# Sums over partitions of the second layer's modulation chunks, issued in the middle of the next chunk

## The chip, the cores and the metric

One core of a Trainium2 chip runs the whole kernel. The metric is the device time of one launch in microseconds (us); three runs of the kernel before gave 2981.88, 2982.76 and 2983.58 us. TensorE is PE here, VectorE is DVE, ScalarE is ACT, GpSimd is POOL, SyncE is SP; SP issues most of the loads from memory.

## The reference, cut to what matters

Two layers over 1024 latent tokens and 256 context tokens of width 1024. Each layer takes six modulation vectors for the latents (from `c`) and six for the context (from `c_ctx`) out of a product of a 1024-vector with a 1024 x 6144 matrix.

```python
def adaln(cond, w, b):
    m = jax.nn.silu(cond) @ w + b
    return jnp.split(m[..., None, :], 6, axis=-1)
...
for i in range(DEPTH):
    sh1, sc1, g1, sh2, sc2, g2 = adaln(c, ada_w[i], ada_b[i])
    csh1, csc1, cg1, csh2, csc2, cg2 = adaln(c_ctx, ada_w[i], ada_b[i])
    hx = modulate(rmsnorm(x, norm1_g[i]), sh1, sc1)
    ...
    x = x + g1 * yx
    x = x + g2 * sq_relu_mlp(modulate(rmsnorm(x, norm2_g[i]), sh2, sc2), mlp_w1[i], mlp_w2[i])
```

In the last layer only two of the context's vectors are needed, so of the second layer's 24 chunks of 256 columns the first 8 are made for both conditions and the other 16 for `c` alone.

## The kernel before, in words

The kernel is one stream of work per engine in an order written out by hand; no scheduler moves anything. The first layer's MLP (`mlp(0, ...)`, about 490 to 1480 us) is where the second layer's modulations are made beside the matmuls.

**The MLP.** Every matmul of it is three (`mm3`, L341 to L343: high x high, high x low, low x high). After three first up-projections it runs in passes. A pass is `down` of two rows of hidden channels, then two `up`s. `down` goes over three blocks of tokens (latents 0 to 511, latents 512 to 1023, the 256 context tokens), in each over 8 output tiles d; a group of 6 matmuls fills one PSUM bank, the banks 2, 3, 4, 5 in turn, and DVE adds each bank into the residual (`xL` for latents, `xC` for context; this is called an eviction below). The PE can therefore be four groups ahead of DVE's evictions and no more. `up` has 24 matmuls for each of the three blocks, in banks 0 and 1, which ACT empties. The weights come through `Stream`: a raw 512 KB load into a tile of ring R (three tiles), a high part by ACT and a low part by POOL into ring W (L333, L337; a split), after which the next raw load is issued.

**Background steps.** `later("ada", ada_dve(1))` hands in a Python generator, and `step()` runs it up to its next `yield`. `down` calls `step()` after every second d, `up` once after each block. So a pass has 18 steps; below they are named by place: a1 to a4 in `down` of the first latents, b1 to b4 in that of the second latents, c1 to c4 in that of the context, u1 to u3 after the three blocks of the first `up`, u4 to u6 after those of the second. What a step issues stands on each engine's queue behind what was issued ahead of it.

**A chunk** (`ada_dve`, L516 to L552) takes 9 steps: (1) take an accumulator from ring Y (three tiles) and load the first half of its weights into a tile of R (L525); (2), (3) DVE multiplies and adds that half into the accumulator, two of four slices in each step (in the trace `Y<-R,k` and `Y<-R,k,Y`, 4 instructions a step for two conditions and 2 for one; DVE instructions of the helpers all have L296); (4) load the second half; (5), (6) the same for it; (7) nothing; (8) the sums over partitions: matmuls of the accumulator with a column of ones into bank 7 (L543, 4 matmuls for two conditions and 2 for one; the trace counts each as two); (9) DVE adds the bias and stores the result (`k<-bank,k`, called the placing below), and once in four chunks POOL makes scale vectors from it (`fin_mod`).

Two chunks of 9 steps are one pass of 18, so each pass looks like the one before. The even chunk has its sums at a4. The odd one has step 1 at b2, steps 2 and 3 at b3 and b4, step 4 at c1, steps 5 and 6 at c2 and c3, and its sums at u1.

R's loads are issued by SP in the order of the program. A load waits until the last reader of the tile it overwrites is done: a DVE instruction where that held modulation weights, a POOL split where it held a raw weight.

Of the kernel before, what the change touches and what calls it, by code (L numbers as in the profile page):

```python
# [13 lines left out]
ALU = mybir.AluOpType  # L14
# [187 lines left out]
class Kern:  # L202
# [312 lines left out]

    def ada_dve(self, layer):  # L516

        nc, I = self.nc, self.I
        for chunk in range(24):
            conds = (0, 1) if chunk < 8 else (0,)  # L520
            n = len(conds)
            acc = self.Y.v(2, 256)
            for kh in range(2):
                w = self.R.v(4, 256)
                nc.sync.dma_start(out=w, in_=I["ada_w"][layer, 512 * kh:512 * kh + 512,  # L525
                                                        256 * chunk:256 * chunk + 256]
                                  .rearrange("(k p) c -> p k c", p=128))
                yield
                for k in range(4):
                    for c in conds:  # L530
                        s = self.cs[:, 4 * kh + k, c:c + 1]
                        if kh + k == 0:
                            self.ts(acc[:, c], w[:, k], s, ALU.mult)
                        else:
                            self.stt(acc[:, c], w[:, k], s, acc[:, c], ALU.mult, ALU.add)
                    if k == 1:
                        yield
                yield
            yield
            ps = self.PS[7]  # L540
            for j in range(2):
                for c in conds:
                    nc.tensor.matmul(ps[:, 2 * j + c:2 * j + c + 1], lhsT=acc[:, c, 128 * j:128 * j + 128],  # L543
                                     rhs=self.ones[:, 0:1], start=True, stop=True)
            yield
            d0 = 2 * chunk % 8
            for c in conds:
                self.tt(self.modc[:, layer, c, chunk // 4, d0:d0 + 2], ps[:, c:c + 3:2],
                        self.adab[:, layer, 2 * chunk:2 * chunk + 2], ALU.add)
            if chunk % 4 == 3:  # L550
                self.fin_mod(layer, chunk // 4, conds)
            yield  # L552


    def exp_small(self, o, x, tmp):
# [1594 lines left out]
```

## Time and profile before

| what | value |
|---|---|
| median of three runs | 2982.76 us (2981.88 to 2983.58) |
| the profiled execution: its time | 2984.72 us |
| the profiled execution: its span | 2982.9 us, mean granted clock 0.984 |
| PE busy | 2868.5 us, 96% |
| DVE busy | 1764.3 us, 59% |
| POOL busy | 1148.5 us, 39% |
| ACT busy | 1028.6 us, 34% |

The span is the time from the first to the last recorded instruction; 1.8 us of the profiled execution's time lie around it. PE is busy nearly always, so a microsecond is won where PE stands idle or where its clock is granted at the lower of its two levels (1.2 and 2.4 GHz; a granted clock of 0.50 is the lower, 1.00 the upper).

### The profile page before, as it was taken

How to read it: one execution, taken by the hardware profiler on the slowest of the kernel's cores; microseconds unless marked ns; L12 is line 12 of the kernel's file. 1: busy time of each engine (PE TensorE's matmuls, PEld its weight loads, DVE VectorE, ACT ScalarE, POOL GpSimd, SP SyncE). 2: the span in 40 equal slices, each digit the busy share in tenths (PEclk: the TensorE clock that was granted, in tenths of full speed). 3: DMA queues.
4: the chain of work that ended last, by engine and by line, in shares of the span. 5: the costliest groups of instructions: out<-in, count | busy, mean ns of one | idle time of the engine just before them, and what ended most of it. 6: DMA issues, size and time to landing. Idle time of an engine off the chain costs nothing.

```text
span 2982.9 us, 39200 instructions
## 1 busy us (share of the span) xinstructions
PE 2868.5 (96%) x15186; PEld 2390.5 (80%) x15186; DVE 1764.3 (59%) x3533; ACT 1028.6 (34%) x1799; POOL 1148.5 (39%) x842
## 2 busy tenths in 40 slices
PE   5899999999999999999999999999999999999999
PEld 2666788788888888888778788999887888888887
DVE  7789867644554454332779847999966322332233
ACT  3342343222122212212334435666644223223221
POOL 5613233422223223323434425787724333333332
PEclk8898999999999999999999999999999999999999
DMA  7265530222212222111155642322222111111111
GB/s 287 90 192 164 189 109 17 64 64 64 71 64 85 73 69 81 62 36 43 40 160 163 159 126 89 101 82 84 77 93 65 54 50 50 50 43 57 44 49 71
DMA packets 179035, 263.30 MB, mean 88 GB/s; under 512 B 8736, under 2 KB 125984, under 8 KB 178336
## 3 DMA queue, kind: packets, MB, share of 16 engines
q1 hardware_dynamic: 168208, 233.53, 25.0%
q0 software_dynamic: 10640, 27.26, 3.0%
q8 instruction: 119, 1.95, 0.3%
q14 instruction: 68, 0.56, 0.1%
HBM read 210.92 MB, written 49.84 MB: 87 GB/s over the span
## 4 chain that ended last, share of the span: by engine, by line
PE 73%; DVE 18%; ACT 3%; DMA 3%; issue 2%; POOL 2%; SPq 0%; DVEq 0%; ACTq 0%; POOLq 0%
PE bank L341 19%; PE bank L342 19%; PE bank L343 19%; PE sc L1686 4%; PE pv L1726 4%; DVE Y L296 3%; DVE T L895 2%; DVE E L296 2%; PE tb L1717 2%; DVE xh L899 2%; DMA R<-in_ada_w_dram 1%; DVE hl L296 1%; DVE S L296 1%; DVE R L296 1%; DVE xL L296 1%
## 5 line engine op out<-in xcount | busy, mean ns | idle before, releaser
L296 DVE SCALAR_TENSOR_TENSOR xL<-bank,k,xL 128x512 f32<-128x512 f32 x544 | 404.5, 749 | 905.0 <-PE bank L343 904.7
L337 POOL TENSOR_TENSOR W<-R,W 128x1024 fp32r<-128x1024 f32 (+1 forms) x138 | 330.6, 2406 | 684.6 <-ACT W L333 395.8
L341 PE MATMUL bank<-H,W 128*128 128x512 f32 (+1 forms) x1280 | 473.5, 370 | 2.2 <-DVE xC L296 2.2
L342 PE MATMUL bank<-H,W 128*128 128x512 f32 (+1 forms) x1280 | 471.0, 368 | 0.0
L343 PE MATMUL bank<-H,W 128*128 128x512 f32 (+1 forms) x1280 | 471.0, 368 | 0.0
L333 ACT CAST W<-R 128x1024 fp32r<-128x1024 f32 (+2 forms) x180 | 178.2, 1009 | 667.8 <-PE bank L343 363.6
L337 POOL TENSOR_TENSOR H<-E,H 128x512 fp32r<-128x512 f32 (+1 forms) x160 | 190.8, 1193 | 476.3 <-ACT H L333 462.3
L341 PE MATMUL bank<-hl,W 128*128 128x512 f32 (+1 forms) x768 | 303.6, 395 | 8.1 <-ACT hl L433 3.8
L342 PE MATMUL bank<-hl,W 128*128 128x512 f32 (+1 forms) x768 | 299.1, 389 | 6.6 <-DVE hl L296 5.6
L343 PE MATMUL bank<-hl,W 128*128 128x512 f32 (+1 forms) x768 | 296.8, 386 | 1.1 <-DVE W L337 1.1
L341 PEld LDWEIGHTS bank<-H,W 128*128 128x128 f32 x1280 | 241.3, 189 | 43.5 <-DVE xC L296 3.4
L343 PEld LDWEIGHTS bank<-H,W 128*128 128x128 f32 x1280 | 241.2, 188 | 40.5
L342 PEld LDWEIGHTS bank<-H,W 128*128 128x128 f32 x1280 | 241.4, 189 | 39.8 <-issue 0.2
L1453 ACT ACTIVATE E<-bank 128x512 f32<-128x512 f32 (+1 forms) x160 | 88.8, 555 | 491.8 <-PE bank L343 491.8
L1691 DVE TENSOR_REDUCE S<-sc 128x1 f32<-128x1280 f32 x128 | 184.2, 1480 | 38.9 <-PE sc L1686 38.9
L341 PEld LDWEIGHTS bank<-hl,W 128*128 128x128 f32 x768 | 148.8, 194 | 59.1 <-issue 19.2
L296 DVE SCALAR_TENSOR_TENSOR Y<-R,k,Y 128x256 f32<-128x256 f32 x224 | 166.4, 773 | 28.3 <-DMA R<-in_ada_w_dram 25.7
L342 PEld LDWEIGHTS bank<-hl,W 128*128 128x128 f32 x768 | 148.5, 193 | 39.2 <-DVE hl L296 11.5
L343 PEld LDWEIGHTS bank<-hl,W 128*128 128x128 f32 x768 | 147.9, 193 | 29.7 <-DVE W L337 1.5
L1686 PE MATMUL sc<-K,W 128*128 128x512 f32 x720 | 167.7, 369 | 0.0
L1726 PE MATMUL pv<-xL,wT 128*128 128x128 f32 x1280 | 155.8, 275 | 0.0
L324 POOL TENSOR_TENSOR R<-R,S 128x896 f32<-128x896 f32 x64 | 107.4, 1678 | 112.0 <-DVE S L296 87.5
(387 smaller groups left out, 5960.4 us busy)
## 6 DMA issues: line engine op xcount, KB each, us to landing
R<-in_w_dram SPq DMA_DIRECT2D x128, 512.0 KB, 3.6
R<-in_ada_w_dram SPq DMA_DIRECT2D x52, 512.0 KB, 3.6
W<-q_d POOLq DMA_DIRECT2D x15, 1024.0 KB, 5.5
A<-in_ada_w_dram SPq DMA_DIRECT2D x24, 512.0 KB, 4.4
hl<-in_ada_w_dram SPq DMA_DIRECT2D x20, 512.0 KB, 9.7
kk_d<-T SPq DMA_DIRECT2D x20, 512.0 KB, 3.2
K<-kk_d POOLq DMA_DIRECT2D x8, 1280.0 KB, 6.2
R<-in_od_in_dram SPq DMA_DIRECT2D x18, 512.0 KB, 3.7
```

Source lines behind the costliest of these rows:

```text
L296: f(**kw)
L324: self.nc.gpsimd.tensor_tensor(out=o, in0=a, in1=b, op=op)
L333: nc.scalar.copy(hi, src)
L337: e.tensor_tensor(out=lo, in0=src, in1=hi.bitcast(F32), op=ALU.subtract)
L341: mm(ps, lhsT=lh, rhs=rh, start=first, stop=False)
L342: mm(ps, lhsT=lh, rhs=rl, start=False, stop=False)
L343: mm(ps, lhsT=ll, rhs=rh, start=False, stop=last)
L895: v.tensor_tensor(out=b.raw(o, [[48, 2], [1, 32]]), in0=self.CAb.raw(64 * d, [[32, 2], [1, 32]]), in1=h.raw(prev[d], [[0, 2], [1, 32]]), o ...
L1453: self.nc.scalar.activation(out=e, in_=ps, func=AF.Relu)
L1686: nc.tensor.matmul(self.SC[i][:, c0:c0 + n], lhsT=Qf[:, e, q0:q0 + 128], rhs=K[:, i, c0:c0 + n], start=e == 0, stop=e == 1)
L1691: nc.vector.tensor_reduce(out=st[:, i, 1:2], in_=self.SC[i][:, 0:1280], axis=AX.X, op=ALU.max, negate=True)
L1726: nc.tensor.matmul(self.PV[:, 0:128], lhsT=it["wT"][:, kt], rhs=heads[h]["v"][:, kt], start=kt == 8, stop=kt == 3)
```

## The change

A chunk's sums and placing are taken out of the chunk and done in the next one. The sums stand at the end of the step after the next chunk's step 3, the placing at the head of the first step that works on the next chunk's second half. The empty step 7 and the two steps that held only the sums and the placing go, one empty step comes at the end, so a chunk has 8 steps and not 9: (1) load, (2), (3) the first half, (4) the sums of the chunk before, (5) load, (6) the placing of the chunk before and the second half's first two slices, (7) the other two, (8) nothing. A 25th turn without work of its own sums and places the last chunk. The instructions are the same ones, as many as before on each engine, with the same operands.

```diff
+        late = None
+
+        def sums(acc, conds):
+            ps = self.PS[7]
+            for j in range(2):
+                for c in conds:
+                    nc.tensor.matmul(ps[:, 2 * j + c:2 * j + c + 1], lhsT=acc[:, c, 128 * j:128 * j + 128],
+                                     rhs=self.ones[:, 0:1], start=True, stop=True)
+
+        def place(chunk, conds):
+            d0 = 2 * chunk % 8
+            for c in conds:
+                self.tt(self.modc[:, layer, c, chunk // 4, d0:d0 + 2], self.PS[7][:, c:c + 3:2],
+                        self.adab[:, layer, 2 * chunk:2 * chunk + 2], ALU.add)
+            if chunk % 4 == 3:
+                self.fin_mod(layer, chunk // 4, conds)
+
+        for chunk in range(25):
...
                 yield
-                for k in range(4):
+                if late and kh:
+                    place(late[0], late[2])
+                    late = None
+                for k in range(4) if chunk < 24 else ():
...
                     if k == 1:
                         yield
                 yield
-            yield
-            ps = self.PS[7]
-            for j in range(2):
-                for c in conds:
-                    nc.tensor.matmul(ps[:, 2 * j + c:2 * j + c + 1], lhsT=acc[:, c, 128 * j:128 * j + 128],
-                                     rhs=self.ones[:, 0:1], start=True, stop=True)
-            yield
-            d0 = 2 * chunk % 8
...
-            yield
+                if late:
+                    sums(late[1], late[2])
+                yield
+            late = (chunk, acc, conds)
```

With 8 steps a chunk and 18 a pass, nine chunks fill four passes, and the places move from pass to pass. The sums of chunks 0 to 8 stand at b4 and u4 of the first pass, b2 and u2 of the second, a4 and c4 of the third, a2, c2 and u6 of the fourth; then it begins anew. All 24 chunks take 198 steps and not 216, so the generator ends one pass earlier.

PE, first pass, around the end of the first `up`'s first block, before (`bank1_7` is the bank of the sums, `Y51_8` the accumulator of chunk 1, `hl` the normed latents, `W12_29` and `W12_30` the two `up`s' weights):

```order
L341 MATMUL bank1_1_61<-hl_47_3675,W12_29_4967 128x512
L342 MATMUL bank1_1_61<-hl_47_3675,W12_29_4967 128x512
L343 MATMUL bank1_1_61<-hl_47_3675,W12_29_4967 128x512
L543 MATMUL bank1_7_67<-k_7_94,Y51_8_5070 128x1 x4
L341 MATMUL bank1_0_60<-hl_48_3679,W12_29_4967 128x512
```

The same sums after the change, on PE around the end of the second `up`'s first block:

```order
L341 MATMUL bank1_0_60<-hl_47_3675,W12_30_5175 128x512
L342 MATMUL bank1_0_60<-hl_47_3675,W12_30_5175 128x512
L343 MATMUL bank1_0_60<-hl_47_3675,W12_30_5175 128x512
L526 MATMUL bank1_7_67<-k_7_94,Y51_8_5050 128x1 x4
L341 MATMUL bank1_1_61<-hl_48_3679,W12_30_5175 128x512
```

Chunk 1's sums moved from u1 to u4, three blocks of `up` later on PE.

DVE, second pass, at the seam of the second latents and the context (b4 to c2), before (`xL` and `xC` rows are evictions, `Y51_10` is chunk 3's accumulator, `R13_52` and `R13_53` its two halves of weights):

```order
L296 SCALAR_TENSOR_TENSOR xL_37_2870<-bank1_4_64,k_9_102,xL_37_2870 128x512
L296 SCALAR_TENSOR_TENSOR xL_37_2870<-bank1_5_65,k_9_102,xL_37_2870 128x512
L296 SCALAR_TENSOR_TENSOR Y51_10_5486<-R13_52_5487,k_11_110,Y51_10_5486 128x256 x4
L296 SCALAR_TENSOR_TENSOR xC_38_2874<-bank1_2_62,k_9_102,xC_38_2874 128x256
L296 SCALAR_TENSOR_TENSOR xC_38_2874<-bank1_3_63,k_9_102,xC_38_2874 128x256
L296 SCALAR_TENSOR_TENSOR xC_38_2874<-bank1_4_64,k_9_102,xC_38_2874 128x256
L296 SCALAR_TENSOR_TENSOR xC_38_2874<-bank1_5_65,k_9_102,xC_38_2874 128x256
L296 SCALAR_TENSOR_TENSOR Y51_10_5486<-R13_53_5539,k_11_110,Y51_10_5486 128x256 x4
```

The same seam after the change:

```order
L296 SCALAR_TENSOR_TENSOR xL_37_2870<-bank1_4_64,k_9_102,xL_37_2870 128x512
L296 SCALAR_TENSOR_TENSOR xL_37_2870<-bank1_5_65,k_9_102,xL_37_2870 128x512
L296 TENSOR_TENSOR k_9_102<-bank1_7_67,k_3_76 128x2 x2
L296 SCALAR_TENSOR_TENSOR Y51_10_5438<-R13_53_5509,k_11_110,Y51_10_5438 128x256 x4
L296 SCALAR_TENSOR_TENSOR xC_38_2874<-bank1_2_62,k_9_102,xC_38_2874 128x256
L296 SCALAR_TENSOR_TENSOR xC_38_2874<-bank1_3_63,k_9_102,xC_38_2874 128x256
L296 SCALAR_TENSOR_TENSOR Y51_10_5438<-R13_53_5509,k_11_110,Y51_10_5438 128x256 x4
L296 SCALAR_TENSOR_TENSOR xC_38_2874<-bank1_4_64,k_9_102,xC_38_2874 128x256
L296 SCALAR_TENSOR_TENSOR xC_38_2874<-bank1_5_65,k_9_102,xC_38_2874 128x256
```

A placing and four accumulator instructions now stand ahead of the first context eviction, and four more ahead of the third; before, four stood ahead of the first and the next four behind the fourth.

DVE, third pass, in the first latents (a2 and the evictions behind it), before:

```order
L296 SCALAR_TENSOR_TENSOR xL_37_2870<-bank1_5_65,k_9_102,xL_37_2870 128x512
L296 SCALAR_TENSOR_TENSOR Y51_11_5694<-R13_58_5797,k_11_110,Y51_11_5694 128x256 x4
L296 SCALAR_TENSOR_TENSOR xL_37_2870<-bank1_2_62,k_9_102,xL_37_2870 128x512
L296 SCALAR_TENSOR_TENSOR xL_37_2870<-bank1_3_63,k_9_102,xL_37_2870 128x512
L296 SCALAR_TENSOR_TENSOR xL_37_2870<-bank1_4_64,k_9_102,xL_37_2870 128x512
```

The same place after the change (`Y51_12` is chunk 5):

```order
L296 SCALAR_TENSOR_TENSOR xL_37_2870<-bank1_5_65,k_9_102,xL_37_2870 128x512
L296 TENSOR_SCALAR Y51_12_5826<-R13_60_5827,k_11_110 128x256 x2
L296 SCALAR_TENSOR_TENSOR Y51_12_5826<-R13_60_5827,k_11_110,Y51_12_5826 128x256 x2
L296 SCALAR_TENSOR_TENSOR xL_37_2870<-bank1_2_62,k_9_102,xL_37_2870 128x512
L296 SCALAR_TENSOR_TENSOR xL_37_2870<-bank1_3_63,k_9_102,xL_37_2870 128x512
L296 SCALAR_TENSOR_TENSOR Y51_12_5826<-R13_60_5827,k_11_110,Y51_12_5826 128x256 x4
```

The end of chunk 4 stood here before; now chunk 5 begins here. Its load (`R13_60`) goes into a tile of R that a raw weight held, and waits for the POOL split of that weight, the one at the head of the pass.

## Rows read from the trace of the kernel before

**Rows 1.** The page: span, instructions; PE busy (share) x instructions, PEld, DVE, ACT, POOL.

```profile
span 2982.9 us, 39200 instructions
PE 2868.5 (96%) x15186; PEld 2390.5 (80%) x15186; DVE 1764.3 (59%) x3533; ACT 1028.6 (34%) x1799; POOL 1148.5 (39%) x842
```

**Rows 2.** PE's waits, 550 to 800, then 800 to 1262: us, times, longest us.

```profile
PE bank L543 <- DVE Y L296: 14.7, 4, 3.7
```

```profile
PE bank L543 <- DVE Y L296: 5.2, 8, 0.7
```

**Rows 3.** PE by pass: window, us, busy (instructions), granted clock, DMA share, GB/s.

```profile
550.50:614.40 63.90, 60.28 (x306) 0.95 0.23 74
...
863.20:920.30 57.10, 56.43 (x299) 1.00 0.24 74
...
1262.40:1317.50 55.10, 55.10 (x291) 1.00 0.13 39
```

**Rows 4.** PE behind the four long waits, the same columns.

```profile
588.48:594.42 5.94, 5.94 (x18) 0.50 0.27 88
594.42:600.00 5.58, 5.58 (x34) 1.00 0.27 97
652.44:659.27 6.83, 6.83 (x20) 0.50 0.24 79
717.30:724.12 6.82, 6.82 (x20) 0.50 0.23 77
782.15:785.56 3.41, 3.41 (x11) 0.50 0.47 154
```

**Rows 5.** PE's timeline: start us, us, instruction, count [idle before <- releaser].

```profile
561.43 0.95 PE L543 MATMUL bank<-k,Y 128*128 128x1 f32 x8
...
573.27 0.28 PE L341 MATMUL bank<-H,W 128*128 128x256 f32 x1
...
573.98 0.28 PE L341 MATMUL bank<-H,W 128*128 128x256 f32 x1
...
588.48 1.86 PE L543 MATMUL bank<-k,Y 128*128 128x1 f32 x8 [3.62 <-DVE Y L296]
```

```profile
1239.70 0.61 PE L543 MATMUL bank<-k,Y 128*128 128x1 f32 x4 [0.67 <-DVE Y L296]
```

**Rows 6.** DVE's timeline in the first pass, the same columns.

```profile
554.52 3.31 DVE L296 SCALAR_TENSOR_TENSOR Y<-R,k,Y 128x256 f32<-128x256 f32 x4 [0.33 <-DMA R<-in_ada_w_dram]
...
565.98 0.21 DVE L296 TENSOR_TENSOR k<-bank,k 128x2 f32<-128x2 f32 x2
...
569.39 0.75 DVE L296 SCALAR_TENSOR_TENSOR xL<-bank,k,xL 128x512 f32<-128x512 f32 x1 [0.61 <-PE bank L343]
570.75 0.75 DVE L296 SCALAR_TENSOR_TENSOR xL<-bank,k,xL 128x512 f32<-128x512 f32 x1 [0.61 <-PE bank L343]
...
574.14 1.67 DVE L296 SCALAR_TENSOR_TENSOR Y<-R,k,Y 128x256 f32<-128x256 f32 x4
575.72 1.66 DVE L296 SCALAR_TENSOR_TENSOR xC<-bank,k,xC 128x256 f32<-128x256 f32 x4
579.46 5.99 DVE L296 SCALAR_TENSOR_TENSOR Y<-R,k,Y 128x256 f32<-128x256 f32 x4 [2.08 <-DMA R<-in_ada_w_dram]
...
586.16 2.67 DVE L296 SCALAR_TENSOR_TENSOR Y<-R,k,Y 128x256 f32<-128x256 f32 x4
```

**Rows 7.** Accumulator instructions, then latent evictions: duration ns min/median/max, first and last start.

```profile
L296 DVE SCALAR_TENSOR_TENSOR Y<-R,k,Y x224: 468/484/2673, 538.2 to 1237.1; 128x256 f32<-128x256 f32 x112
```

```profile
L296 DVE SCALAR_TENSOR_TENSOR xL<-bank,k,xL x192: 733/750/753, 552.1 to 1227.9; 128x512 f32<-128x512 f32 x192
```

**Rows 8.** POOL's timeline: weight splits in the first pass and at the second's head.

```profile
580.24 4.92 POOL L337 TENSOR_TENSOR W<-R,W 128x1024 fp32r<-128x1024 f32 x2 [23.88 <-ACT W L333]
```

```profile
617.01 2.40 POOL L337 TENSOR_TENSOR W<-R,W 128x1024 fp32r<-128x1024 f32 x1 [0.27 <-ACT W L333]
```

**Rows 9.** The page's loads: count, KB, median us to landing.

```profile
R<-in_ada_w_dram SPq DMA_DIRECT2D x52, 512.0 KB, 3.6
```

**Rows 10.** Waits 550 to 1262 of SP's queue, then 760 to 1250 of ACT.

```profile
SPq L149 <- DVE Y L296: 43.5, 19, 3.0
```

```profile
ACT W L333 <- PE bank L343: 229.0, 9, 25.8
```

More of the change, by code (lines that the diff above doesn't have):

```diff
@@ L518, in ada_dve @@
         nc, I = self.nc, self.I
-        for chunk in range(24):
+        late = None
[13 more added lines that the diff above has]
+        for chunk in range(25):
             conds = (0, 1) if chunk < 8 else (0,)
-            n = len(conds)
-            acc = self.Y.v(2, 256)
+            if chunk < 24:
+                acc = self.Y.v(2, 256)
             for kh in range(2):
[L524 to L527, printed above, removed]
+                if chunk < 24:
+                    w = self.R.v(4, 256)
+                    nc.sync.dma_start(out=w, in_=I["ada_w"][layer, 512 * kh:512 * kh + 512,
+                                                            256 * chunk:256 * chunk + 256]
+                                      .rearrange("(k p) c -> p k c", p=128))
                 yield
-                for k in range(4):
+                if late and kh:
+                    place(late[0], late[2])
+                    late = None
+                for k in range(4) if chunk < 24 else ():
                     for c in conds:
@@ L538, in ada_dve @@
                 yield
-            yield
-            ps = self.PS[7]
-            for j in range(2):
-                for c in conds:
-                    nc.tensor.matmul(ps[:, 2 * j + c:2 * j + c + 1], lhsT=acc[:, c, 128 * j:128 * j + 128],
-                                     rhs=self.ones[:, 0:1], start=True, stop=True)
-            yield
-            d0 = 2 * chunk % 8
[L547 to L551, printed above, removed]
-            yield
+                if late:
+                    sums(late[1], late[2])
+                yield
+            late = (chunk, acc, conds)
     def exp_small(self, o, x, tmp):
```

## The prediction

> **What bounds the kernel now.** I read the page first: PE is busy for 2868.5 of 2982.9 us [rows 1], so only PE's idle time and its clock can give anything. Then PE's waits over the stretch in which the chunks are made. One line stands there: the sums (L543) waited 12 times for DVE's accumulator, four times for 14.7 us together and eight times for 5.2 us [rows 2], 19.9 us in all. Then the windows by pass: the first pass takes 63.90 us at a granted clock of 0.95, a pass whose chunks have one condition 57.10 us at 1.00, and a pass without chunks 55.10 us, busy all the time [rows 3]. So the chunks cost PE 8.8 us in a pass with two conditions and 2.0 us in one with one. Last, PE's timeline at one of the long waits: 3.62 us of idle time, then the eight records of the sums take 1.86 us where the same eight took 0.95 us at 561.43 us [rows 5]. The window behind it shows why: granted clock 0.50, the lower level, for 5.94 us, and 1.00 again after it [rows 4].
>
> DVE's timeline tells where the 3.6 us come from [rows 6]. Four accumulator instructions at b4 end at 575.8 us, four context evictions follow, and then the second half of the odd chunk waits for its load, which could only start when b4's four had freed a tile of R. It begins at 579.46 us, needs 5.99 us for four instructions that take 1.67 us elsewhere, since two weight splits run on POOL from 580.24 us for 4.92 us [rows 8], and the last four start at 586.16 us. PE got to the sums at u1 3.6 us too early. With one condition the same chain is half as long, and the wait is 0.67 us [rows 5].
>
> **What the change removes.** (1) The 12 waits: the sums of a chunk now stand five steps behind the chunk's last DVE step. The shortest such stretch is chunk 5's, whose last DVE step is b3 and whose sums stand at c4: PE has two latent groups between, at 1.36 us (evictions that wait for PE follow each other at 569.39 and 570.75 us [rows 6]), and eight context groups at 0.71 us (573.27 to 573.98 us [rows 5]), 8.4 us. DVE was late by 3.7 us at most [rows 2]. So I take all 19.9 us as gone. (2) The low clock behind the long waits. From the sums on it lasts 5.94, 6.83, 6.82 and 3.41 us [rows 4], 23.0 us at half speed, which is 11.5 us lost. It began each time with a wait of 3.6 to 3.7 us, and not once with the eight short ones (the pass at 863.20 us has 1.00 [rows 3]), so it goes with the long waits. Together 31.4 us.
>
> What stays: the sums themselves, 24 of them, with as many instructions as before. A pass with one condition is 57.1 - 55.1 - 0.65 (5.2 us by 8 waits) = 1.35 us dearer than one without chunks, two sums' worth of 0.7 us. They interrupt PE wherever they stand, so nothing is won or lost by where; and they still write bank 7, which no MLP matmul uses.
>
> **What it moves.** Loads: the 48 loads are the same ones, but each now stands elsewhere among the raw weights' loads in SP's queue. What hides them: SP's raw loads waited up to 3.0 us for DVE to free a tile of R, and ACT's splits were nevertheless held by PE, up to 25.8 us, and not by loads [rows 10]. A raw load can be late by that much before PE sees it, so I cost this at nothing; if the cover went, PE would wait for a weight, with a half clock behind it. The placing on DVE now waits for the sums of two steps ago. Behind it in DVE's queue stand accumulator instructions and evictions; two steps of PE lie between, so it finds its bank ready. POOL's `fin_mod` waits for the placing of chunks 7 and 19 alone, with weight splits queued behind it, and PE is then at c4 and u6, where DVE is at most a few short instructions behind: nothing.
>
> What is new is where the accumulator instructions meet the evictions, since PE can be only four groups ahead. A group of four takes 1.58 us (574.14 to 575.72), a context eviction 0.4 us, a latent one 0.75 us [rows 6]. Two places with two conditions come out short:
> - Second pass, the seam b4/c1 (chunk 3). PE starts the context at time 0. In the trace the last latent eviction is done 0.87 us later (573.27 [rows 5] to 574.14 [rows 6]). Then the placing 0.2 us [rows 6], four accumulator instructions 1.58 us, and the first context eviction ends at 3.1 us. PE's fifth group wants that bank at 4 x 0.71 = 2.84 us: a wait of 0.3 us. Four more accumulator instructions put the third eviction's end at 5.55 us, and PE's seventh group wants it at 4.5 us: 1.0 us. Sum 1.3 us.
> - Third pass, a2 (chunk 5). The load waits for POOL's split. In the second pass that ends 5.0 us after the pass's start (617.01 + 2.40 [rows 8], start 614.40 [rows 3]); the load lands 3.6 us later [rows 9], four instructions make it 10.2 us, the eviction 10.95 us. PE's ninth group wants it at 8 x 1.36 = 10.9 us: 0.1 us. The next eviction and four more instructions make it 13.2 us and the third eviction 13.95 us, where PE's eleventh group wants its bank at 13.6 us: 0.3 us. Sum 0.4 us.
>
> With one condition these groups have half the length, and the same working leaves no wait. New waits: 1.7 us. No row shows either place. The lower bound is nothing; below nothing it can't be, since in the present order the waits of this stretch name the sums alone [rows 2] and no eviction. The upper bound is a half clock behind each of the two, 3.4 us each by the longest of rows 4, so 8.5 us. I take 1.7 us: the short waits of rows 2 are the nearest in length, and they cost their own length.
>
> The accumulator instructions stretch beside POOL: 484 ns in the median, 2673 ns at most, while the latent evictions stay within 733 to 753 ns [rows 7]. The Trainium skill (SBUF — State Buffer, section "SBUF: two separate sides") has a rule that speaks against moving them into `down`: the port pair that DVE shares with GpSimd is locked for a whole instruction, and a DVE instruction with two SBUF inputs stands still until the GpSimd one is done. The trace agrees: four took 5.99 us against POOL's 4.92 us. By that rule every group at a1 or a2 could be held for a split's 2.40 us with evictions behind it; if that came on top at both places above, the sum would be 4.8 us higher, where by the rows the split has ended before chunk 5's load starts.
>
> **The sum.** Against the profiled execution, 2984.72 us (span 2982.9 us and 1.8 us around it): -19.9 - 11.5 + 1.7 = -29.7, so 2955.0 us. That execution lies 2.0 us above the median of the runs, so on their scale 2953 us.
>
> **The rivals.**
> - New short waits bring the clock down. The 1.3 us at chunk 3 or the 0.4 us at chunk 5 is enough, or a third place falls short: 3.4 us for each, 2953 + 3.4 to 2953 + 10. For it: the new waits stand beside other broken stretches. Against it: eight waits of 0.65 us left the clock at 1.00 [rows 2, 3]. The Trainium skill (TensorE: Matmul & The Clock Gate, section "A second HAM failure mode: psum-queue depth-cycling") says that frequent small gaps between groups of matmuls, as banks are cycled, can make the clock swing; no row here shows it.
> - Only part of the gain: the one-condition waits or the low clock come back at other places. 2964 to 2976 us, by keeping the 11.5 us or more.
> - The change doesn't do what it says: DVE is still writing the accumulator when PE comes to the new place. It decides from a lag of 8.4 us on; the rows show 3.7. Then the 12 waits and their clock stay: within 6 us of 2983.
> - Slower: DVE's queue becomes PE's limit in `down`. Place: a group of four at a1 to b4 with evictions behind it. PE has four groups, 5.45 us; less the eviction ahead and the one behind, a group may take some 3.8 us. The group at 554.52 us took 3.31 us beside POOL [rows 6] and cost PE nothing; one of 5.99 us there would cost 2.2 us and, as with rows 4, some 3 us of clock. If two places in each of 11 passes crossed it, 22 x 5 = 110 us against 31: about 3060 us; to end slower by 0.2% it takes eight such places. Against it: POOL's long pairs of splits run at c and u1, and only one split at the head of `down`.
>
> **How the numbers follow.** Forecast 0.64, clock at new waits 0.20, part of the gain 0.07, no effect 0.05, slower 0.04. The range: 2949 us (no new wait, 2951.4, less the scatter of the runs) to 2964 us (both new places with a half clock, 2960, and one more of 3.6 us); it leaves out the last three. Measured here, 0.2% or 6 us is about what can be told from no change: faster 0.91, same 0.05, slower 0.04.
>
> **What would show it.** In the changed kernel's profile the line of the sums waiting for DVE is gone from PE's waits. The granted clock is 1.00 in every pass with chunks, and a pass with two conditions takes 58 to 59 us. A line of PE waiting for DVE's `xC` or `xL` appears, with 1 to 3 us in total, the largest at the seam of the second pass. I am wrong if that line holds 6 us or more, if the clock falls behind it, or if PE waits for `W`.

## The result and the profile after

The changed kernel takes 2952.75 us in the median of four runs (2950.45 to 2954.23), the kernel before 2982.32 us in four: a ratio of 0.9889, interval 0.9877 to 0.9902. It is 1.1% faster; 2953 us was forecast. The profiled execution took 2952.55 us against 2984.72 us, 32.2 us less.

The page of the changed kernel, the first two lines as in [rows 1]:

```profile
span 2950.8 us, 39233 instructions
PE 2854.7 (97%) x15186; PEld 2384.6 (81%) x15186; DVE 1732.3 (59%) x3533; ACT 1028.4 (35%) x1799; POOL 1149.0 (39%) x842
```

The engines run the same instructions as before (the 33 more in the count are not on these five lines). PE is busy 13.8 us less, for the most part since the matmuls behind the long waits no longer run slowly, and the span is 32.1 us shorter, so some 18 us of PE's idle time went.

PE's waits between 549 and 1229 us, the stretch of the passes with chunks, which answer to [rows 2]: engine, line, what it waited for, us in all, times, longest.

```profile
PE bank L341 <- DVE xL L296: 1.1, 1, 1.1
PE bank L341 <- DVE xC L296: 0.7, 1, 0.7
```

No line of the sums is left. Two waits for evictions came in their place, 1.8 us together.

PE by pass, the columns of [rows 3]: window, us, busy (instructions), granted clock, DMA share, GB/s.

```profile
549.60:608.10 58.50, 57.41 (x305) 1.00 0.24 82
608.10:666.40 58.30, 57.54 (x307) 1.00 0.26 82
666.40:723.30 56.90, 56.90 (x306) 1.00 0.24 75
723.30:780.60 57.30, 57.30 (x310) 1.00 0.26 83
780.60:836.80 56.20, 56.20 (x299) 1.00 0.24 76
...
1173.60:1228.70 55.10, 55.10 (x290) 1.00 0.14 39
```

The clock is 1.00 in each of them, where the first four passes had 0.95 to 0.97; the fourth of the kernel before, which [rows 3] leaves out, was this:

```profile
743.30:806.20 62.90, 59.19 (x306) 0.97 0.21 68
```

A pass with two conditions takes 56.9 to 58.5 us and not 62.9 to 64.6 us, one with one condition 56.0 to 56.4 us and not 57.0 to 57.1 us, and the generator ends a pass earlier.

The stretch from the first pass to the end of the passes, 14 of them, in the kernel before and in the changed one:

```profile
550.52:1372.57 822.05, 802.10 (x4161) 0.99 0.21 67
```

```profile
549.65:1338.91 789.26, 787.42 (x4162) 1.00 0.22 70
1338.91:2950.80 1611.89, 1584.13 (x8256) 0.99 0.27 80
```

The passes are 32.8 us shorter. Ahead of them 0.9 us is gained, behind them 1.6 us lost (2982.9 - 1372.57 = 1610.3 us before), which is less than the runs of one kernel differ by. So the whole result lies where the change is.

### The profile page after: what moved, and what is told of

Read it like the earlier page. It is cut to its first block, busy times and chain, and to the rows that moved or that the text cites. A ratio compares the mean times of both kernels' runs of the same rounds, so it can differ in the third digit from the quotient of the medians.

```text
span 2950.8 us, 39233 instructions
## 1 busy us (share of the span) xinstructions
PE 2854.7 (97%) x15186; PEld 2384.6 (81%) x15186; DVE 1732.3 (59%) x3533; ACT 1028.4 (35%) x1799; POOL 1149.0 (39%) x842
## 4 chain that ended last, share of the span: by engine, by line
PE 81%; DVE 9%; issue 3%; ACT 3%; POOL 2%; DMA 2%; SPq 0%; DVEq 0%; ACTq 0%; POOLq 0%
PE bank L341 22%; PE bank L342 21%; PE bank L343 21%; PE sc L1698 4%; PE pv L1738 4%; PE tb L1729 2%; DVE E L296 2%; DVE hl L296 1%; DVE S L296 1%; POOL E L324 1%; POOL E L427 1%; DVE S L1703 1%; DVE W L337 1%; PE bank L1573 1%; DMA hl<-in_ada_w_dram 1%
## 5 line engine op out<-in xcount | busy, mean ns | idle before, releaser
L341 PE MATMUL bank<-hl,W 128*128 128x512 f32 (+1 forms) x768 | 299.2, 390 | 8.0 <-ACT hl L433 3.7
L342 PE MATMUL bank<-hl,W 128*128 128x512 f32 (+1 forms) x768 | 296.0, 385 | 8.2 <-DVE hl L296 7.3
L343 PE MATMUL bank<-hl,W 128*128 128x512 f32 (+1 forms) x768 | 293.4, 382 | 1.1 <-DVE W L337 1.1
L341 PEld LDWEIGHTS bank<-hl,W 128*128 128x128 f32 x768 | 146.2, 190 | 58.6 <-issue 19.2
L342 PEld LDWEIGHTS bank<-hl,W 128*128 128x128 f32 x768 | 146.3, 190 | 40.2 <-DVE hl L296 12.9
L343 PEld LDWEIGHTS bank<-hl,W 128*128 128x128 f32 x768 | 146.1, 190 | 29.0 <-DVE W L337 1.5
L1738 PEld LDWEIGHTS pv<-xL,wT 128*128 128x128 f32 x1280 | 149.2, 192 | 0.1
```

The lines of the kernel that those rows point to most:

```text
L341: mm(ps, lhsT=lh, rhs=rh, start=first, stop=False)
L342: mm(ps, lhsT=lh, rhs=rl, start=False, stop=False)
L343: mm(ps, lhsT=ll, rhs=rh, start=False, stop=last)
L1738: nc.tensor.matmul(self.PV[:, 0:128], lhsT=it["wT"][:, kt], rhs=heads[h]["v"][:, kt], start=kt == 8, stop=kt == 3)
```

## The experiments

The theory: the sums came too early for DVE, and what was lost is PE's idle time in front of them and the lower clock behind it. The rivals: the gain comes from the shorter chunk, whose places drift from pass to pass; or the low clock has a cause of its own.

**The same chunk, sums one step later (plus1).** The kernel before with one step more ahead of the sums and the placing moved to the head of the next chunk, so the chunk keeps its 9 steps and its places:

```diff
             yield
+            yield
             ps = self.PS[7]
             for j in range(2):
...
             yield
             d0 = 2 * chunk % 8
...
                 self.fin_mod(layer, chunk // 4, conds)
-            yield
```

> The kernel before with one thing moved: a chunk keeps its 9 steps and every accumulator instruction its place, but the sums stand one step later (step 9 and not 8) and the placing at the head of the next chunk. PE comes to the odd chunk's sums one block of up later, 24 x 0.227 = 5.5 us, where the waits were 3.7 us at most. Theory (the gain is that the sums are late enough): the line of sums waiting for DVE is gone, the clock is 1.00 in every pass with chunks, no new wait for an eviction: 2982.3 - 19.9 - 11.5 = 2951, down to 2947 if a sum that doesn't wait also costs less by itself. Rival (the gain comes from the 8-step chunk, whose places drift from pass to pass): 2978 to 2986, with the sums still waiting.

2954.78 us, against 2988.2 us for the kernel before on the same chip: ratio 0.9887 (0.987 to 0.9903), the whole gain. In its trace PE waits for nothing between 551 and 1262 us. Its windows of a pass with two conditions, of the eight passes with one condition together, and of a pass without chunks:

```profile
608.90:666.10 57.20, 57.20 (x307) 1.00 0.24 74
```

```profile
780.43:1228.91 448.48, 448.48 (x2371) 1.00 0.24 74
```

```profile
1228.90:1284.00 55.10, 55.10 (x290) 1.00 0.12 39
```

One step of lateness is enough; neither the 8 steps nor the drift is needed.

**The drift without the lateness (early8).** The kernel before without its empty step 7: 8 steps a chunk, sums right behind the last DVE step.

```diff
                 yield
-            yield
             ps = self.PS[7]
```

> The kernel before with the empty step 7 taken out: a chunk has 8 steps and its places drift as in the changed kernel, but the sums stay in their own chunk, one step behind its last DVE step. Theory (lateness): sums that follow a DVE step in the context part or beside POOL's splits still wait, 8 us or more in the line of sums waiting for DVE, and long waits bring low clock: 2962 to 2990. Rival (drift of the places): the line under 2 us and 2949 to 2957.

2979.37 us, ratio 0.9969 (0.9957 to 0.9981). PE's waits between 554 and 1262 us, then the three longest and the next one on PE's timeline, and the window behind the first:

```profile
PE bank L542 <- DVE Y L296: 16.2, 12, 2.7
```

```profile
586.47 1.22 PE L542 MATMUL bank<-k,Y 128*128 128x1 f32 x8 [2.68 <-DVE Y L296]
...
751.71 1.23 PE L542 MATMUL bank<-k,Y 128*128 128x1 f32 x8 [1.69 <-DVE Y L296]
...
774.76 0.61 PE L542 MATMUL bank<-k,Y 128*128 128x1 f32 x4 [2.31 <-DVE Y L296]
...
1006.39 0.61 PE L542 MATMUL bank<-k,Y 128*128 128x1 f32 x4 [2.37 <-DVE Y L296]
```

```profile
588.10:591.50 3.40, 3.40 (x14) 0.50 0.37 137
```

The sums wait as often as before, 16.2 us in all and not 19.9 us, and three spells of low clock are left in the passes (at 588, 776 and 1008 us), behind the three longest waits, and not four longer ones. So an 8-step chunk with early sums does not bring the gain.

It does not price the drift by itself. Without the empty step the sums stand right behind the last DVE step, one step nearer to it than in the kernel before. The run below named minus1 has its sums as near, but keeps 9 steps a chunk and so does not drift: its sums wait 83.1 us, and its ratio is 1.0301 where this run has 0.9969, on another chip. With sums that early the drift is thus worth some 3%; the longest wait is 2.7 us here and 8.0 us there. An 8-step chunk whose sums stand as far behind the last DVE step as in the kernel before was not run, so it stays open how much of the gain the drift alone would have brought. That it is not needed is shown by plus1 and late9.

**The low clock alone (filler).** The kernel before with matmuls that need nothing ahead of the four sums that waited long:

```diff
             ps = self.PS[7]
+            if chunk in (1, 3, 5, 7):
+                hh = self.hv(0, 512)[0]
+                for i in range(16):
+                    nc.tensor.matmul(self.PS[6], lhsT=self.identr, rhs=hh[:, i % 8], start=True, stop=True)
```

> The kernel before with 16 matmuls of 128x512 that need nothing (3.64 us by 0.227 each, into bank 6, never read) put on PE just ahead of the sums of chunks 1, 3, 5 and 7, so PE is busy where it stood idle. The wait's length stays, as matmuls. Theory (the low clock follows PE's idle time): the granted clock is 1.00 behind all four, the two-condition passes are 3.4, 3.4, 3.4 and 1.7 us shorter: 2982.3 - 11.5 = 2970.8 (2968 to 2974). Rival (the low clock comes from the sums or from what DVE and POOL do there): 0.50 behind them as before, 2980 to 2985.

2980.25 us, ratio 0.9972 (0.9961 to 0.9984). The first filler on PE's timeline, and the first pass:

```profile
585.95 3.91 PE L544 MATMUL bank<-hl,k 128*128 128x512 f32 x16
```

```profile
551.80:613.30 61.50, 61.34 (x322) 1.00 0.25 77
```

All four passes together, in the kernel before and in this run:

```profile
550.50:806.20 255.70, 240.99 (x1217) 0.95 0.22 68
```

```profile
551.80:797.50 245.70, 245.37 (x1281) 1.00 0.24 71
```

The clock stays at 1.00 with the sums, the accumulators and POOL's splits all where they were. It was PE's idle time that brought it down. The first pass is 2.4 us shorter than before [rows 3], and all four 10 us, for 11.5 us expected: the fillers cost somewhat more than the waits that they filled (the first filler and the gap behind it 4.05 us, for a wait of 3.62 us). By the ratio the kernel gained 0.3%, 8 us; the 2968 to 2974 us of the expectation was on the other chip's scale, where 0.9972 is 2974 us, its upper end.

**Both (late9).** The changed kernel with an empty step more in each chunk, so its places no longer drift:

```diff
                 yield
+            yield
             late = (chunk, acc, conds)
```

> The changed kernel with one empty step more at the end of each chunk: 9 steps again, the same places in each pass, sums in the middle of the next chunk. Theory (lateness): sums never wait, clock 1.00, and the accumulator instructions stand at b3, b4, c3, c4 (odd chunk) and a2, a3 (even chunk), so no four of them stand ahead of the context's first or third eviction: 2947 to 2953. Rival (drift): 2975 to 2985.

2952.39 us, ratio 0.9884 (0.9869 to 0.9899). One wait is left in its passes, at the first pass, and a later pass with two conditions is as short as the changed kernel's shortest:

```profile
PE bank L341 <- DVE xL L296: 0.9, 1, 0.9
```

```profile
665.20:722.10 56.90, 56.90 (x306) 1.00 0.25 75
```

**The other direction (minus1).** The kernel before with the empty step behind the sums and not ahead of them, so PE comes to them a step earlier:

```diff
                 yield
-            yield
             ps = self.PS[7]
...
             yield
+            yield
             d0 = 2 * chunk % 8
```

> The kernel before with the sums one step earlier (step 7 and not 8), the rest in place: the other direction of the same dose. PE comes to the odd chunk's sums at c4 and not at u1, one block of up or 5.5 us earlier, and DVE ends when it did. Theory (lateness and clock): 12 waits, four of 3.7 + 5.5 = 9.2 us and eight of 0.65 + 5.5 = 6.1 us, 85 us in all, and now a half clock behind each, 12 x 3.4 us: 2982 + 65 + 29 = 3077 (3050 to 3090). Rival (the wait is set by something that moves with PE, a buffer or a bank): waits about as before, 2980 to 2995.

3072.49 us against 2982.3 us, ratio 1.0301 (1.028 to 1.0321). PE's waits between 550 and 1350 us, and the windows behind a wait with two conditions and one with one:

```profile
PE bank L542 <- DVE Y L296: 83.1, 16, 8.0
```

```profile
584.00:594.20 10.20, 5.51 (x17) 0.50 0.49 154
860.50:867.30 6.80, 5.02 (x14) 0.50 0.70 231
```

The waits came to 83.1 us where 85 us was expected, and there is now low clock behind the one-condition waits too. The total is nearer than its parts. The eight one-condition waits are 6.0 us, as expected. The four long ones are 7.1 to 8.0 us and not 9.2 us, mostly because in those passes the even chunk's sums, which the expectation left out, now wait too, 0.7 to 1.6 us, and PE comes to the odd chunk's sums that much later. Those four waits make the count 16 and not 12. One step either way is worth 90 us on one side and 30 us on the other.

**What the sums cost (plus1_nosums).** plus1 without the sums' matmuls:

```diff
             ps = self.PS[7]
-            for j in range(2):
-                for c in conds:
-                    nc.tensor.matmul(ps[:, 2 * j + c:2 * j + c + 1], lhsT=acc[:, c, 128 * j:128 * j + 128],
-                                     rhs=self.ones[:, 0:1], start=True, stop=True)
```

> The run plus1 without the sums' matmuls; bank 7 keeps what the first layer left, so the second layer's modulations are not the reference's, and the time is read for the sums alone. In plus1 a pass with chunks took 57.17 us for two conditions and 56.06 us for one, against 55.10 us without chunks. Theory (what is left is the sums themselves, 1.03 us for two conditions and 0.48 us for one): every pass 55.10 us, 16 us below plus1. Rival (part of it is DVE, POOL or the loads disturbing PE): passes between 55.3 and 57.

2940.22 us in one run, 13.5 us below plus1 on the same chip (2953.68 us), where 16 us was expected; by the passes below it is some 15 us over the twelve. Its pass with two conditions and its pass with one:

```profile
608.70:664.00 55.30, 55.30 (x291) 1.00 0.25 77
829.70:884.80 55.10, 55.10 (x291) 1.00 0.24 77
```

All that plus1's one-condition passes have above 55.10 us are the sums, 0.48 us each; with two conditions it is 0.95 us each, and the 0.2 us a pass that is left then has no cause shown.

**plus1 and the changed kernel on one chip.**

> plus1 beside the changed kernel on one chip. By the passes of the two traces (787.5 us against 789.3 us over 14 passes) it is 1.8 us faster, the changed kernel's two short waits; by rounds that can't be told: both 0.988 to 0.990 of the kernel before.

> The changed kernel itself, beside plus1 on one chip: 0.988 to 0.990 of the kernel before; its waits of PE for xL and xC come back at the same two places, in the first and the second pass, if they are a matter of order and not of chance.

0.9904 (0.9887 to 0.992) and 0.9906 (0.9891 to 0.992): no difference that can be told, and both just above the 0.988 to 0.990 that was expected, which their intervals reach. The changed kernel's waits in the passes were these:

```profile
PE bank L341 <- DVE xL L296: 0.9, 1, 0.9
PE bank L341 <- DVE xC L296: 0.7, 1, 0.7
```

They stand in the same two places as in its first trace, so they come from the order; plus1 has none, and its passes are 1.8 us shorter, which the runs are too few to show.

## Why the prediction was right

**The waits, 19.9 us.** Right. plus1 and minus1 show the cause: only the step at which the sums stand differs (with the placing behind them), and the waits vanish, or grow from 0.67 to 6.0 us with one condition, about the 5.5 us of a block of `up`.

**The low clock, 11.5 us.** Right in cause: the fillers kept the clock up with everything else in place. The size fits too, 10 us by the fillers, which cost a little themselves. The rival that the new short waits bring the clock down failed: the longest, 1.1 us, left the first pass at 1.00. The swing that the Trainium skill describes (TensorE: Matmul & The Clock Gate, section "A second HAM failure mode: psum-queue depth-cycling") was not seen in any pass of the changed kernel.

**The sums, at no change.** This step failed in its size. "Nothing is won or lost by where" holds for sums that don't wait; one that waits costs more than its wait. The prediction took both sums of a one-condition pass at 0.7 us; one that does not wait is 0.48 us by plus1_nosums. The kernel before, over the same eight one-condition passes as plus1 above:

```profile
806.22:1262.37 456.15, 450.91 (x2370) 1.00 0.23 73
```

That is 7.7 us more than plus1's 448.48 us, and the eight waits are 5.2 us of it [rows 2]. The other 2.5 us are 0.3 us for each sum that found PE idle. PE's timeline in the kernel before shows where most of it lies, first around sums that did not wait, then around sums that did:

```profile
816.90 0.39 PE L343 MATMUL bank<-H,W 128*128 128x512 f32 x1
817.13 0.50 PE L543 MATMUL bank<-k,Y 128*128 128x1 f32 x4
817.49 0.49 PE L341 MATMUL bank<-H,W 128*128 128x512 f32 x1
```

```profile
1238.65 0.39 PE L343 MATMUL bank<-hl,W 128*128 128x512 f32 x1
1239.70 0.61 PE L543 MATMUL bank<-k,Y 128*128 128x1 f32 x4 [0.67 <-DVE Y L296]
1240.17 0.48 PE L341 MATMUL bank<-hl,W 128*128 128x512 f32 x1
```

The accumulator is what these matmuls load as weights, and the weight loads of the two groups begin here:

```profile
816.90 0.64 PEld L543 LDWEIGHTS bank<-k,Y 128*128 128x128 f32 x4
```

```profile
1239.70 0.52 PEld L543 LDWEIGHTS bank<-k,Y 128*128 128x128 f32 x4 [1.09 <-DVE Y L296]
```

Without a wait the sums follow 0.23 us behind the start of the matmul ahead, which itself lasts 0.39 us, and their weight load has run under it. With a wait that overlap of 0.16 us is lost, and as the weight load starts only at the wait's end, the next `up` follows 0.47 us behind the sums' start and not 0.36 us. Together that is 0.27 us.

Over all 14 passes, plus1 (787.50 us, no wait) is 34.5 us shorter than the kernel before, of which the waits and the low clock were to be 31.4 us: 3.1 us are left for the 12 sums, 2.5 us of them the eight above. It closes the account of the changed kernel's passes too: 31.4 + 3.2 - 1.8 = 32.8 us, as measured, where 29.7 us was forecast; the 3.2 us there is what the account leaves.

**The new waits, 1.7 us.** The total was right, 1.8 us, but partly by luck: one place was overrated, one forecast place has no wait, and one that was not forecast has the longest. At the seam of the second pass it is 0.67 us, not 1.3 us. DVE's timeline there, and PE's wait:

```profile
631.88 1.66 DVE L296 SCALAR_TENSOR_TENSOR Y<-R,k,Y 128x256 f32<-128x256 f32 x4
633.46 0.87 DVE L296 SCALAR_TENSOR_TENSOR xC<-bank,k,xC 128x256 f32<-128x256 f32 x2
634.24 1.67 DVE L296 SCALAR_TENSOR_TENSOR Y<-R,k,Y 128x256 f32<-128x256 f32 x4
635.82 2.05 DVE L296 SCALAR_TENSOR_TENSOR xC<-bank,k,xC 128x256 f32<-128x256 f32 x5
```

```profile
636.36 0.39 PE L341 MATMUL bank<-H,W 128*128 128x256 f32 x1 [0.67 <-DVE xC L296]
```

The third context eviction ends 0.5 us after 635.82 us and PE goes on at once, as worked out; the first came just in time, so the wait of 0.3 us ahead of it fell away, and the rest were tenths. The other wait was forecast for chunk 5, where there is none, and came at the same place of chunk 0, in the first pass:

```profile
553.10 2.39 POOL L337 TENSOR_TENSOR W<-R,W 128x1024 fp32r<-128x1024 f32 x1
```

```profile
555.52 0.38 SPq L544 DMA_DIRECT2D R<-in_ada_w_dram  x1
```

```profile
559.39 1.68 DVE L296 SCALAR_TENSOR_TENSOR Y<-R,k,Y 128x256 f32<-128x256 f32 x4 [3.35 <-DMA R<-in_ada_w_dram]
```

```profile
561.78 0.50 PE L341 MATMUL bank<-H,W 128*128 128x512 f32 x1 [1.09 <-DVE xL L296]
```

The mechanism is the one that was told for chunk 5: a load that waits for POOL's split, a group of four behind it, an eviction behind that. In the first pass the split ends 5.8 us after the pass's start and not 5.0 us, and the prediction left out chunk 0, whose second half moved from a1 to a2. At chunk 5 the load was in DVE's way for 2.17 us, and PE's four groups just covered it; the group of four behind it took 1.32 us (up to 676.28 us) and not 1.58 us:

```profile
674.96 0.62 DVE L296 TENSOR_SCALAR Y<-R,k 128x256 f32<-128x256 f32 x2 [2.17 <-DMA R<-in_ada_w_dram]
```

**The rule on the shared ports.** Groups of four beside a split were stretched as by the Trainium skill's rule (SBUF — State Buffer, section "SBUF: two separate sides"), but none of them held PE up, and the 4.8 us that the rule could have added did not come. The group at the second pass's a1 shows it, 2.87 us beside a split where four took 1.67 us at 634.24 us, with no wait on PE:

```profile
610.75 2.40 POOL L337 TENSOR_TENSOR W<-R,W 128x1024 fp32r<-128x1024 f32 x1 [0.27 <-ACT W L333]
```

```profile
611.75 2.87 DVE L296 SCALAR_TENSOR_TENSOR Y<-R,k,Y 128x256 f32<-128x256 f32 x4
```

**The placing.** This step failed, without a price. The prediction had it find its bank ready, since two steps of PE lie between. DVE's waits over the passes:

```profile
DVE k L296 <- PE bank L526: 35.0, 6, 8.5
```

In `up` nothing holds DVE to PE's pace, since ACT empties the banks there. So DVE came to the placing long before PE had made the sums, six times. Behind it stood only accumulator instructions, whose own sums are five steps away, so PE lost nothing.

**The loads, at nothing.** Right: PE waits for no weight in the passes.

Of the signs that were named, the line of the sums is gone, the clock is 1.00 and the new waits are 1.8 us in all. Two missed: the largest new wait stands in the first pass and not at the seam of the second, and a pass with two conditions took 56.9 to 58.5 us, not 58 to 59 us.

The sum was 2.5 us short of the profiled execution's 32.2 us: 3.2 us for the sums that no longer wait, less 0.7 us outside the passes. The range's low end, 2949 us, had room for it. By the medians the kernel gained 29.6 us, which is the forecast; the runs behind each of these medians differ by 3 to 4 us, so that it came within 1 us is in part luck.

## What to carry to other kernels

Work of one engine that is fed by another belongs where the feeder is done by the latest row, not where it is done on average: here one step of an in-order queue, moved, was worth 30 us, and the same step the other way cost 90 us. Price such a wait with what follows it, since the half clock behind four long waits cost nearly as much as those waits. And follow an order that drifts through every place that it visits, the first turn too; the one wait that was missed stood in the turn that looked most like before.

## What the runs showed of the hardware that was not expected

A small matmul group that finds PE idle costs about 0.3 us over its wait and its own 0.48 us: the overlap with the matmul ahead is lost, and its weight load no longer runs ahead. In early8 the waits of 2.3, 2.4 and 2.7 us were each followed by 3.4 us of low clock, those of up to 1.7 us by none; nor were the waits of 0.7 us in the kernel before and of 1.1 us in the changed one.
